# A hybrid attention and linear-attention block: low-rank weights loaded inside the gk unit, operand splits tied to their weight groups, thirteen bridging products, one more raw tile

## The chip, the cores and the metric

The kernel runs on one core of a Trainium2 chip. The metric is the device time of one execution in microseconds; lower is better. The core has five engines with instruction queues of their own: PE (matrix products), DVE (vector), ACT (activations, also copies and casts), POOL, and SP, which here only issues DMA transfers. They meet only through semaphores, and each queue is worked off in order, so an instruction that waits holds back all that stands behind it on its engine.

## The reference

One encoder layer over 512 tokens of width 2048. A normalised and modulated input goes through one projection; its columns feed a dilated window attention (16 heads of 64) and a bidirectional gated linear attention (GLA, 4 heads). Both branches are gated, concatenated and projected back:

```python
mod = jax.nn.silu(c) @ w_cond[layer] + b_cond[layer]
shift, scale, gate = jnp.split(mod, 3, axis=-1)
h = rms_norm(x) * (1.0 + scale[:, None]) + shift[:, None]
proj = h @ w_in[layer]
aq, ak, av, ag, gq, gk, gv, gg, lr_f, lr_b = jnp.split(proj, PROJ_SPLITS, axis=-1)
...                       # dilated attention of aq, ak, av in three patterns, merged
a_out = att.reshape(B, S, ATT_WIDTH) * jax.nn.silu(ag)
log_g_f = jax.nn.log_sigmoid(lr_f @ gla_gate_up_fwd[layer] + gla_gate_bias_fwd[layer]) / GLA_GATE_NORM
...                       # the same backward; chunked GLA of gq, gk, gv in both directions
g_out = rms_norm(o_fwd + o_bwd).reshape(B, S, GLA_WIDTH) * gla_norm_gain[layer] * jax.nn.silu(gg)
y = jnp.concatenate([a_out, g_out], axis=-1) @ w_out[layer]
x = x + gate[:, None] * y
return rms_norm(x) * final_gain
```

All of it is float32. `lr_f` and `lr_b` are the low-rank columns, 32 in all, from which the decay of the GLA is made.

## The kernel before, in words

**Split products.** A float32 product is made of three faster ones. Each weight tile and each activation tile is split into a high part (a rounding copy on ACT, names ending in `h` or `_hi`) and a low part (the difference, on DVE, ending in `l` or `_lo`). `three` (L230 to L232) issues high x high, high x low and low x high into one sum, so most of PE's work is rows of L230, L231 and L232.

**Stages, in order of time.** (1) Start, to about 107 us: while the conditioning weights (`cb`) and the first projection weights (`rawa`) arrive, `silu(c)` is spread over all partitions by small products on `pc` (L299). `warm` (L296) issues products on a constant tile `hot` whose results nobody reads: 5 before those products, 6 after them. Then come the first real products (`sta`, L591 for the first two of 16 blocks of 128 rows of the contraction, `three` after that); block k needs `h_hi` and `h_lo` of k (L534 on ACT, L537 on DVE), which need the sum over `cb` of k on DVE (L328). (2) Units `qk2`, `qk4`, `qk6`, `gk`: each projects a further group of columns, in 8 groups of weights, and runs the attention of four heads beside it, as "side work" given as pairs of a place (0 to 1 of the unit) and a function. A place of 1 or more spills into the next unit. (3) The value unit (`ps_gv`, weights `V0` to `V27`), whose products follow Strassen's scheme with seven instead of eight block products; `low_rank` (L1312, L1313) and the first GLA head run beside it. (4) Units `ag0`, `ag1`, `gg0`, `gg1` with the other GLA heads. (5) The output projection: two column pairs, seven products each (P1, P7, P6, P4, P5, P3, P2), every product in four weight groups, weights `O0` to `O55`. Its operands are A11, S3, S2, A22, S1, S4 and A12, which are sums and differences of parts of `cat[0..3]` and are split into high and low (`halves`, L1458 on ACT and L1459 on DVE).

**What sets the order.** PE stands in program order. The other engines' instructions are placed by a scheduler at build time; `tc.issue_after(x)` forbids it to place an instruction ahead of x, and a tile pool with n buffers makes the n-th next user of a tag wait until the oldest is released. The names below are used in what follows:

- `lrb` is the tile with the low-rank weights (L1303, a DMA issued by SP); `lrs` its split (L1306 on ACT, L1307 on DVE). `upr`/`ups` (L1320, L1326, L1327) are the up-projection of the decay and its split.
- `pth` and `ptl` are the split transposed attention weights (L888, L889; L906 and L908 for a rest block of 32 rows), `o` the attention values (L915), `gkt` the copies of the gk unit's sums out of PSUM (L1299).
- `GLA_FIRST` holds the places of the ten pieces of GLA head 0 in the value unit; pieces 7 and 8 are `outs(0)` and `outs(1)` (products `go`, L1123), piece 9 is `norm` (products `gn`, L1137, L1138).
- `to_s1`, `to_s2`, `to_s4` (L1471, L1474, L1477, all on DVE) turn parts of `cat` into S1, S2 and S4 in place.
- `later(pair, prod, g, go)` puts `go` into group g of a product of the output projection, ahead of its matrix products. `last["hi"]` and `last["lo"]` are the newest weight split on ACT and on DVE.
- `out_tile` gives the raw weight tiles of the output: even ones from the common ring of four, odd ones from `OUT_DEEP` on from a ring of three in the pool `op`.

Of the kernel before, what the change touches and what calls it, by code (L numbers as in the profile page):

```python
# [10 lines left out]
F32 = mybir.dt.float32  # L11
# [7 lines left out]
P = 128  # L19
S = 512  # L20
D = 2048
KT = D // P
# [96 lines left out]
TOKENS = [slice(256 * c + a, 256 * c + 256, 2) for a in range(2) for c in range(2)]  # L119

GLA_AT = (0.01, 0.02, 0.33, 0.46, 0.46, 0.56, 0.64, 0.76, 0.76, 0.88)
GLA_FIRST = (0.3, 0.38, 0.55, 0.62, 0.775, 0.81, 0.86, 0.9, 0.92, 0.97)

SUMS_IN = {"ag0": 8, "ag1": 8, "gg0": 8}

# [66 lines left out]
def block_kernel(ctx: ExitStack, tc: tile.TileContext, a: dict):  # L192
    nc = tc.nc
# [14 lines left out]
    def T2(name, dt=F32, parts=P):  # L208
        return t2.tile([parts, 512], dt, tag="t2", name=name)
# [34 lines left out]
    def small_inputs():  # L244
        nc.scalar.dma_start(cin, a["c"])
        nc.scalar.dma_start(bcond, a["bcond"])
# [4 lines left out]
    def cond_load(k, e):  # L251

        cb = B8(f"cb{k}_{e}", [2048])
        n = 4 if k == e == 0 else 1
        for z in range(n):
            w = 2048 // n
            nc.sync.dma_start(cb[:, w * z:w * z + w], a["wm"][k, e, :, w * z:w * z + w])
        cond_tiles[k, e] = cb
# [18 lines left out]
    def half_load(z):  # L277
        if not z:
            start_w["a", 0] = RAW("rawa0", [1024])
        c = slice(512 * z, 512 * z + 512)  # L280
        nc.sync.dma_start(start_w["a", 0][:, c], a["w_sa"][0, :, 0, c])
# [11 lines left out]
    def warm(n):  # L293

        for _ in range(n):
            mm(psw, hot[:, :P], hot, start=True, stop=True)  # L296
# [4 lines left out]
    with tc.manual_schedule(engines=PLANNED):  # L301
        small_inputs()
        cond_load(0, 0)
        half_load(0)
        x_load(0)
        half_load(1)
        nc.scalar.preload_act_table_set("silu_and_others")
        nc.vector.memset(hot.bitcast(F32), 1.0)
        nc.vector.memset(epst, EPS)
        nc.vector.memset(ch.bitcast(F32), 0.0)  # L310
        nc.vector.memset(sel.bitcast(F32), 0.0)
        nc.gpsimd.memset(cl.bitcast(F32), 0.0)
        warm(5)

        nc.vector.tensor_copy(ch[:4], cin[:, :512])
        act(sel[:4], cin[:, 512:], AF.Copy)
        tt(cl[:4], cin[:, :512], ch[:4].bitcast(F32), op=ALU.subtract)

        nc.vector.tensor_scalar(bcond[:, 16:32], bcond[:, 16:32], 1.0, None, op0=ALU.add)
        for j in range(4):  # L320
            spread(j, ch, True)
            spread(j, cl, False)
            act(sb[:, 512 * j:512 * j + 512], pcs[j], AF.Silu)
        warm(6)

    def cond_sum(dst, w, with_, init):

# [37 lines left out]
    raws, wts, low, last = {}, {}, set(), {}  # L365
# [27 lines left out]

    def out_tile(s, name):
        if s % 2 and s >= OUT_DEEP:
            return op.tile([P, 2, 512], F32, tag="raw", bufs=3, name=name)
        return RAW(name, [2, 512])

    second = {}
# [108 lines left out]
    part = cst.tile([P, 3], F32, tag="part", name="part")  # L508
# [146 lines left out]
    for z in range(2):  # L655
        c = slice(512 * z, 512 * z + 512)
# [36 lines left out]
    for k in range(2):  # L693
        for z in range(2):
            for e in (0, 2, 1):
                name = ("mm", "a", k, 7) if (z, e) == (1, 1) else ("m", k, z, e)
# [3 lines left out]
    for i in range(n):  # L700
        if i > 15:
            mm_task(i)
        st, k, j = chain[i]
# [14 lines left out]
    for i in range(n, 2 * n):  # L718
        mm_task(i)
        st, k, j = chain[i]  # L720
# [3 lines left out]
    for w in range(4):  # L724
        for kt in range(4):
            j, g = w // 2 * 4 + kt, w % 2
# [285 lines left out]
    def gla_head(h):  # L1012
# [135 lines left out]

        at = GLA_AT if h else GLA_FIRST
        return list(zip(at, [gates(0), gates(1), turn(0), turn(1), states(0), states(1), att,  # L1150
# [8 lines left out]
    def unit(name, natural, side=(), lr=None):  # L1159
        side = sorted(spill + list(side) + block_sums(name), key=lambda x: x[0])  # L1160
        spill[:] = [(at - 1, go) for at, go in side if at >= 1]
        side = [x for x in side if x[0] < 1]
        ps = [PJ(f"ps_{name}_{i}") for i in range(4)]
        pos, tick, ticks = 0, 0, 64
        for g in range(KT // 2):
            i0 = gi[name, g]
            split_hi(i0)
            split_hi(i0 + 1)
            for ahead in (2,) if name in SUMS_IN or name == "gg1" else (2, 3):
                fetch(i0 + ahead)  # L1170
            split_lo(i0)
            hi, lo = wts[i0]
            for i in range(4):
                for kk in range(2):
                    k = 2 * g + kk
                    rh, rl = h_hi[:, k, :], h_lo[:, k, :]
                    if natural:
                        t = slice(i * P, i * P + P)
                        cw = slice(kk * 512, kk * 512 + 512)
                        three(ps[i], rh[:, t], rl[:, t], hi[:, cw], lo[:, cw], k == 0, k == KT - 1)  # L1180
                    else:
                        c = slice(kk * 512 + i * P, kk * 512 + i * P + P)
                        three(ps[i], hi[:, c], lo[:, c], rh, rl, k == 0, k == KT - 1)
                    tick += 1
                    if tick % 8 == 2:
                        split_lo(i0 + 1)
                    while pos < len(side) and side[pos][0] * ticks <= tick:
                        urgent(side[pos][1])
                        pos += 1
                if lr is not None:  # L1190
                    lr(4 * g + i)
        while pos < len(side):
            urgent(side[pos][1])
            pos += 1
        return ps
# [93 lines left out]
    for n, p in (("qk2", 0), ("qk4", 2), ("qk6", 4)):  # L1289
        ps = unit(n, False, attention((p, p + 1)) + ([(0.05, shift_row)] if p == 2 else []))  # L1290
        for q in range(2):
            qk_evict(p + 2 + q, ps[2 * q], ps[2 * q + 1])

    ps = unit("gk", False, attention((6, 7)))
    kp_.close()
    gs = mid.enter_context(tc.tile_pool(name="gs", bufs=1, reuse_waits="tile"))
    gla["k"] = B8("gkt", [4, 512])
# [1 line left out]
        act(gla["k"][:, i, :], ps[i], AF.Copy)  # L1299


    lrb = T2("lrb")
    nc.sync.dma_start(lrb.rearrange("p (k c) -> p k c", k=KT), a["w_lr"][0])  # L1303
    lrs = gp.tile([P, KT, 2, 32], F32R, tag="g", name="lrs")
    lrb3 = lrb.rearrange("p (k c) -> p k c", k=KT)
    act(lrs[:, :, 0, :], lrb3, AF.Copy)  # L1306
    tt(lrs[:, :, 1, :], lrb3, lrs[:, :, 0, :].bitcast(F32), op=ALU.subtract)  # L1307
    plr = PA("plr")
# [126 lines left out]
    for j in range(2):  # L1435
        ps = unit(f"ag{j}", False, gla_head(1 + j) + some_sums(f"ag{j}"))
        gate_evict(ps, cat[j], f"a{j}", vbias[:, 4 * j:4 * j + 4])
    ps = unit("gg0", False, gla_head(3) + some_sums("gg0"))
# [5 lines left out]
    def part(z, c):  # L1444

        return cat[z][:, :, half[c]]
# [6 lines left out]
    def halves(name, z, src):  # L1453

        hi, lo = (t[:, 4 * z:4 * z + 4, :] for t in ops[name])

        def go():
            act(hi, src, AF.Copy)  # L1458
            tt(lo, src, hi.bitcast(F32), op=ALU.subtract)  # L1459
        return go  # L1460
# [9 lines left out]
    def to_s1(z):  # L1470
        tt(part(z, 1), part(2 + z, 1), part(z, 1), op=ALU.subtract)  # L1471

    def to_s2(z):
        stt(part(z, 0), part(z, 1), -1.0, part(z, 0), op0=ALU.mult, op1=ALU.subtract)  # L1474

    def to_s4(z):
        tt(part(z, 0), part(2 + z, 0), part(z, 0), op=ALU.add)  # L1477
# [3 lines left out]
            (0.65, lambda: to_s1(0)), (0.8, lambda: to_s2(0))]  # L1481
    ps = unit("gg1", False, side + some_sums("gg1"))
    gate_evict(ps, cat[3], "g1")
    to_s1(1)
    to_s2(1)
    mid.close()
    op = ctx.enter_context(tc.tile_pool(name="op", bufs=1, reuse_waits="tile"))
    for e in "hl":
# [145 lines left out]
    def later(pair, prod, g, go):  # L1634
        todo.setdefault((pair, prod, g), []).append(go)

    def product(pair, prod, ps, first, last, rows=(0, 1)):

        ah, al = ops[with_[prod]]
        for g in range(4):  # L1640
            s = (pair * len(OUT_ORDER) + OUT_ORDER.index(prod)) * 4 + g
            i0 = gi["O", s]
            ahead = 0 in rows
            if ahead:
                split_hi(i0)
                split_hi(i0 + 1)
                for n in (2, 3, 4, 5):
                    fetch(i0 + n)
                whole(i0 + 2)
                split_lo(i0)  # L1650
                for go in todo.get((pair, prod, g), ()):
                    go()
            wh, wl = wts[i0]
            for n in rows:
                t = slice(P * n, P * n + P)
                for kk in range(2):
                    k = 2 * g + kk
                    c = slice(512 * kk, 512 * kk + 512)
                    three(ps[n], ah[:, k, t], al[:, k, t], wh[:, c], wl[:, c],
                          first and k == 0, last and k == 7, not first)  # L1660
                if ahead and n == 0:
                    split_lo(i0 + 1)

    def a12():
        operand("A12", [B8(f"A12{e}", [4, 512], F32R) for e in "hl"])

    for z in range(2):
        later(0, "P1", 2 * z, halves("S2", z, part(z, 0)))
        later(0, "P7", 2 * z, halves("A22", z, part(2 + z, 1)))
        later(0, "P6", 2 * z, halves("S1", z, part(z, 1)))  # L1670
        later(0, "P6", 2 * z + 1, lambda z=z: (to_s4(z), halves("S4", z, part(z, 0))()))
    later(0, "P4", 0, a12)
    for z in range(2):
        later(0, "P4", 1 + 2 * z, lambda z=z: halves("A12", z, part(2 + z, 0))())
# [133 lines left out]
```

## Time and profile before

| | |
|---|---|
| median of 3 runs | 905.48 us (905.13 to 906.01) |
| the profiled execution | 907.22 us, of which the span from first to last instruction is 905.4 us |
| mean granted TensorE clock | 0.996 |
| PE busy | 890.0 us of the span (98%) |
| DVE, ACT, POOL busy | 731.2, 491.6, 125.9 us |
| DMA | 242.33 MB, mean 268 GB/s |

In the rows of the profile a time stands in microseconds from the span's start, then the duration, the engine (PEld is PE's weight load, SPq the queue of SP), the line, the operation, the tiles as out<-in, their shape, the number of instructions put together (x4), and in brackets the idle time of the engine ahead of the row with what ended it. The start of the next product tells the pace of PE: products overlap, and the duration of one is longer than the step to the next.

### The profile page before, as it was taken

How to read it: one execution, taken by the hardware profiler on the slowest of the kernel's cores; microseconds unless marked ns; L12 is line 12 of the kernel's file. 1: busy time of each engine (PE TensorE's matmuls, PEld its weight loads, DVE VectorE, ACT ScalarE, POOL GpSimd, SP SyncE). 2: the span in 40 equal slices, each digit the busy share in tenths (PEclk: the TensorE clock that was granted, in tenths of full speed). 3: DMA queues.
4: the chain of work that ended last, by engine and by line, in shares of the span. 5: the costliest groups of instructions: out<-in, count | busy, mean ns of one | idle time of the engine just before them, and what ended most of it. 6: DMA issues, size and time to landing. Idle time of an engine off the chain costs nothing.

```text
span 905.4 us, 12339 instructions
## 1 busy us (share of the span) xinstructions
PE 890.0 (98%) x4159; PEld 739.2 (82%) x4159; DVE 731.2 (81%) x1220; ACT 491.6 (54%) x841; POOL 125.9 (14%) x219
## 2 busy tenths in 40 slices
PE   8999999999999999999999999999999999999996
PEld 6888788888888888887778888888888888888885
DVE  7998799878989989888568668595787559797687
ACT  5554533466655745655657554373664248455454
POOL 0000000023323333243000101112020100000001
PEclk9999999999999999999999999999999999999999
DMA  9999489398798898998778879778796988777863
GB/s 342 401 411 363 186 344 367 134 306 226 202 266 273 247 265 247 249 298 223 232 260 255 311 206 308 206 249 262 231 279 208 275 286 289 282 288 249 289 238 154
DMA packets 65547, 242.33 MB, mean 268 GB/s; under 512 B 9190, under 2 KB 11526, under 8 KB 55883
## 3 DMA queue, kind: packets, MB, share of 16 engines
q1 hardware_dynamic: 58724, 199.23, 61.5%
q0 software_dynamic: 6464, 42.01, 19.4%
q8 instruction: 33, 0.54, 0.2%
q10 hardware_dynamic: 296, 0.30, 0.1%
q14 instruction: 30, 0.25, 0.1%
HBM read 224.64 MB, written 51.47 MB: 305 GB/s over the span
## 4 chain that ended last, share of the span: by engine, by line
PE 91%; DVE 3%; ACT 2%; DMA 2%; issue 1%; SPq 0%; DVEq 0%; ACTq 0%
PE ps_qk L230 5%; PE ps_qk L232 5%; PE ps_qk L231 5%; PE g L232 4%; PE g L230 4%; PE g L231 4%; PE stb L232 3%; PE stb L231 3%; PE stb L230 3%; PE ps_ag L232 3%; PE ps_ag L230 3%; PE ps_ag L231 3%; PE o L915 3%; PE sta L230 3%; PE sta L231 3%; PE sta L232 3%
## 5 line engine op out<-in xcount | busy, mean ns | idle before, releaser
L864 POOL TENSOR_SCALAR p<-p,st 128x32 f32<-128x32 f32 (+2 forms) x108 | 59.8, 565 | 159.9 <-DVE st L854 91.2
L328 DVE CUSTOM_DVE_ANT_0 cb<-cb,sb,c_bcond 128x2048 f32<-128x2048 f32 (+1 forms) x32 | 73.4, 2295 | 1.9 <-DMA cb<-in_wm 1.6
L851 ACT ACTIVATE p<-p,st 128x416 f32<-128x416 f32 x64 | 41.0, 641 | 49.2 <-DVE st L847 42.3
L429 POOL DMA_DIRECT2D T<-in_w_o x32 | 23.2, 725 | 159.4 <-ACT V2h L493 14.8
L888 ACT ACTIVATE pth<-t 128x384 fp32r<-128x384 f32 x64 | 31.0, 485 | 19.8 <-PE t L882 11.1
L889 DVE TENSOR_TENSOR ptl<-t,pth 128x384 fp32r<-128x384 f32 x64 | 35.2, 551 | 5.2 <-ACT pth L888 3.7
L882 PE MATMUL t<-c_ident,p 128*128 128x128 f32 x192 | 31.3, 272 | 0.0
L882 PEld LDWEIGHTS t<-c_ident,p 128*128 128x128 f32 x192 | 24.3, 139 | 7.9
L847 DVE CUSTOM_DVE_ANT_0 p<-s,g,st 128x256 f32<-128x256 f32 x64 | 27.7, 432 | 1.8
L847 DVE CUSTOM_DVE_ANT_0 p<-s,g 128x160 f32<-128x160 f32 x64 | 23.5, 367 | 4.2 <-PE s L840 3.5
L328 DVE CUSTOM_DVE_ANT_0 rawg<-rawg,crow,gate 128x1024 f32<-128x1024 f32 x16 | 20.4, 1279 | 4.0 <-DMA rawg<-in_wg 4.0
L1581 POOL TENSOR_SCALAR x<-x,rn 128x512 f32<-128x512 f32 x2 | 2.3, 1167 | 148.5 <-ACT rn L1570 148.5
L429 POOL DMA_DIRECT2D T3V<-in_w_gv x8 | 5.5, 687 | 125.1 <-ACT qk21h L493 118.7
L839 PE MATMUL s<-ks,qh 128*128 128x416 f32 x64 | 22.6, 353 | 0.0
L906 ACT ACTIVATE pth<-r 32x128 fp32r<-32x128 f32 x64 | 17.2, 269 | 9.9 <-PE r L899 4.5
L840 PE MATMUL s<-ks,ql 128*128 128x416 f32 x64 | 22.4, 350 | 0.0
L1091 ACT ACTIVATE sq<-st,sc 128x256 f32<-128x256 f32 x24 | 12.2, 506 | 18.6 <-DVE st L1081 10.0
L328 DVE CUSTOM_DVE_ANT_0 rawg<-rawg,crow,c_bcond 128x1024 f32<-128x1024 f32 x16 | 20.3, 1279 | 0.5 <-DVE g L1028 0.5
L429 POOL DMA_DIRECT2D T<-T x16 | 9.1, 571 | 79.9 <-ACT V8h L493 12.9
L915 PE MATMUL o<-pth,vv 128*128 128x512 f32 (+1 forms) x64 | 15.9, 369 | 2.2 <-DVE pth L908 1.1
L466 DVE TENSOR_TENSOR raw_O<-raw_O,raw_P 128x1024 f32<-128x1024 f32 x8 | 9.8, 1225 | 10.1 <-DMA raw_O<-in_w_o 7.8
L568 ACT ACTIVATE h_hi<-xt,shift 128x512 fp32r<-128x512 f32 x16 | 11.5, 721 | 10.3 <-DVE shift L328 9.5
(1661 smaller groups left out, 3151.6 us busy)
## 6 DMA issues: line engine op xcount, KB each, us to landing
cb<-in_wm SPq DMA_DIRECT2D x31, 1024.0 KB, 9.3
T<-in_w_o POOLq DMA_DIRECT2D x32, 512.0 KB, 6.5
rawg<-in_wg SPq DMA_DIRECT2D x32, 512.0 KB, 5.4
raw_O<-in_w_o SPq DMA_DIRECT2D x32, 512.0 KB, 4.6
raw_qk<-in_w_qk SPq DMA_DIRECT2D x24, 512.0 KB, 4.9
raw_O<-T SPq DMA_DIRECT2D x24, 512.0 KB, 5.0
rawb<-in_w_sb SPq DMA_DIRECT2D x16, 512.0 KB, 8.9
rawv<-in_wv SPq DMA_DIRECT2D x16, 512.0 KB, 5.6
```

What stands on the lines that cost most here:

```text
L230: mm(ps, lh, rh, start=first, stop=False, skip_group_check=more)
L231: mm(ps, ll, rh, start=False, stop=False, skip_group_check=more)
L232: mm(ps, lh, rl, start=False, stop=last, skip_group_check=more)
L328: return nc.vector.tensor_tensor_reduce(out=w, in0=w, in1=with_, op0=ALU.mult, op1=ALU.add, scale=1.0, scalar=init, accum_out=dst)
L429: move = nc.gpsimd.dma_start(dst, src, max_dma_last_dim=8192, **how).ins
L847: top = nc.vector.tensor_tensor_reduce(out=t[:, lo:hi], in0=ps[:, lo:hi], in1=gt[h][:, at:at + 2 * (hi - lo) - 1:2], op0=ALU.add, op1=ALU.min,
L851: act(t, t, AF.Exp, bias=st[:, 0:1], scale=-1.0, accum_out=st[:, 1:2])
L864: last["pool"] = nc.gpsimd.tensor_scalar(to, of, st[:, 2:3], 1.0, op0=ALU.mult, op1=ALU.mult).ins
L882: nc.tensor.transpose(pk[:, n_ * P:n_ * P + P], t[:, first_ + kt * P:first_ + kt * P + P], ident)
L888: act(hi, src, AF.Copy)
L889: tt(lo, src, hi.bitcast(F32), op=ALU.subtract)
L915: mm(po[:, P * a0:P * a1], vv[h // 4][:, c, h % 4, :], pt[:, at:at + (a1 - a0 - 1) * step + 1:step, :], start=n_ == z == 0, stop=False, sk ...
```

## The change

Five edits:

1. `warm(6)` becomes `warm(13)`: thirteen products on `hot` follow the spread products instead of six.
2. `lrb` is loaded by a piece of side work at place 0.88 of the gk unit, not behind the unit.
3. In `GLA_FIRST`, `outs(0)` moves from 0.9 to 0.91 and `outs(1)` from 0.92 to 0.93.
4. In the output, `to_s1(1)` and `to_s2(1)` move from ahead of the output into groups 2 and 3 of P1, and the splits of S2, A22, S1 and S4 go through `in_turn`, which places them behind the newest weight split of both engines; the two splits of S2 move to group 1 of P1 and group 1 of P7.
5. The ring of odd raw tiles has four buffers instead of three.

```diff
-GLA_FIRST = (0.3, 0.38, 0.55, 0.62, 0.775, 0.81, 0.86, 0.9, 0.92, 0.97)
+GLA_FIRST = (0.3, 0.38, 0.55, 0.62, 0.775, 0.81, 0.86, 0.91, 0.93, 0.97)
...
-        warm(6)
+        warm(13)
...
-            return op.tile([P, 2, 512], F32, tag="raw", bufs=3, name=name)
+            return op.tile([P, 2, 512], F32, tag="raw", bufs=4, name=name)
...
-    ps = unit("gk", False, attention((6, 7)))
+    lrb = []
+
+    def lr_load():
+        lrb.append(T2("lrb"))
+        nc.sync.dma_start(lrb[0].rearrange("p (k c) -> p k c", k=KT), a["w_lr"][0])
+
+    ps = unit("gk", False, attention((6, 7)) + [(0.88, lr_load)])
...
-    lrb = T2("lrb")
-    nc.sync.dma_start(lrb.rearrange("p (k c) -> p k c", k=KT), a["w_lr"][0])
...
     gate_evict(ps, cat[3], "g1")
-    to_s1(1)
-    to_s2(1)
...
+    def in_turn(pair, prod, g, *fns):
+
+        def go():
+            with tc.issue_after(last["hi"]), tc.issue_after(last["lo"]):
+                for fn in fns:
+                    fn()
+        later(pair, prod, g, go)
...
+    in_turn(0, "P1", 2, lambda: to_s1(1))
+    in_turn(0, "P1", 3, lambda: to_s2(1))
     for z in range(2):
-        later(0, "P1", 2 * z, halves("S2", z, part(z, 0)))
-        later(0, "P7", 2 * z, halves("A22", z, part(2 + z, 1)))
-        later(0, "P6", 2 * z, halves("S1", z, part(z, 1)))
-        later(0, "P6", 2 * z + 1, lambda z=z: (to_s4(z), halves("S4", z, part(z, 0))()))
+        in_turn(0, ("P1", "P7")[z], 1, halves("S2", z, part(z, 0)))
+        in_turn(0, "P7", 2 * z, halves("A22", z, part(2 + z, 1)))
+        in_turn(0, "P6", 2 * z, halves("S1", z, part(z, 1)))
+        in_turn(0, "P6", 2 * z + 1, lambda z=z: to_s4(z), halves("S4", z, part(z, 0)))
```

The edits leave PE's order as it was but for the seven further `warm` products and the place of `go`. What the scheduler makes of them on the other engines, at the places of which the prediction speaks:

**End of the gk unit, SP.** `S` is a store of a token sum, `raw_V` the weight tiles V5 and V6. Before:

```order
L391 DMA raw_V_4347<-in_w_gv 128x1024
L1320 DMA upr<-in_up 128x1024
L1220 DMA S_1506<-S_4100 128x512
L391 DMA raw_V_4384<-in_w_gv 128x1024
L1303 DMA lrb<-in_w_lr 128x512
```

And now:

```order
L391 DMA raw_V_4354<-in_w_gv 128x1024
L1324 DMA upr<-in_up 128x1024
L1220 DMA S_1513<-S_4107 128x512
L1298 DMA lrb<-in_w_lr 128x512
L391 DMA raw_V_4391<-in_w_gv 128x1024
```

The load of `lrb` has changed places with the load of V6, which waits for a raw buffer.

**The same place, ACT.** Before:

```order
L1299 ACTIVATE gkt_4325<-ps_gk_3671 128x512
L888 ACTIVATE pth<-t_4277 128x3x128
L1299 ACTIVATE gkt_4325<-ps_gk_3672 128x512
L888 ACTIVATE pth<-t_4286 128x3x128
L906 ACTIVATE pth<-r_4296 32x128 x2
L1306 ACTIVATE lrs<-lrb 128x16x32
L888 ACTIVATE pth<-t_4306 128x3x128
L906 ACTIVATE pth<-r_4296 32x128 x2
L1299 ACTIVATE gkt_4325<-ps_gk_3673 128x512
L1326 ACTIVATE ups<-upr 128x1024
L1299 ACTIVATE gkt_4325<-ps_gk_3674 128x512
```

And now:

```order
L1305 ACTIVATE gkt_4334<-ps_gk_3678 128x512
L888 ACTIVATE pth<-t_4286 128x3x128
L1310 ACTIVATE lrs<-lrb 128x16x32
L1305 ACTIVATE gkt_4334<-ps_gk_3679 128x512
L888 ACTIVATE pth<-t_4295 128x3x128
L1330 ACTIVATE ups<-upr 128x1024
L906 ACTIVATE pth<-r_4305 32x128 x2
L888 ACTIVATE pth<-t_4315 128x3x128
L1305 ACTIVATE gkt_4334<-ps_gk_3680 128x512
L1305 ACTIVATE gkt_4334<-ps_gk_3681 128x512
L906 ACTIVATE pth<-r_4305 32x128 x2
```

`lrs` stands three rows earlier, `ups` has moved ahead of the last attention tile, and the second pair of `pth<-r` stands behind two more `gkt` copies.

**Start of the output, DVE.** `cat<-cat,sgg` are the gates of the last unit; of the rows of shape 128x4x256, the one that reads `cat_5127` is `to_s4(0)` and the one that reads `cat_5990` is `to_s1(1)` (now the one with `cat_5997`); the SCALAR_TENSOR_TENSOR is `to_s2(1)`. Before:

```order
L1202 TENSOR_TENSOR cat_5990<-cat_5990,sgg_6780 128x512
L1459 TENSOR_TENSOR c_l<-cat_1611,c_h 128x1024
L1202 TENSOR_TENSOR cat_5990<-cat_5990,sgg_6783 128x512
L1477 TENSOR_TENSOR cat_1611<-cat_5127,cat_1611 128x4x256
L1471 TENSOR_TENSOR cat_3027<-cat_5990,cat_3027 128x4x256
L477 TENSOR_TENSOR O2l<-raw_O_6807,O2h 128x1024
L1474 SCALAR_TENSOR_TENSOR cat_3027<-cat_3027 128x4x256
L477 TENSOR_TENSOR O3l<-raw_O_6809,O3h 128x1024
```

And now:

```order
L1202 TENSOR_TENSOR cat_5997<-cat_5997,sgg_6787 128x512
L1202 TENSOR_TENSOR cat_5997<-cat_5997,sgg_6790 128x512
L477 TENSOR_TENSOR O2l<-raw_O_6812,O2h 128x1024
L1463 TENSOR_TENSOR c_l<-cat_1618,c_h 128x1024
L1475 TENSOR_TENSOR cat_3034<-cat_5997,cat_3034 128x4x256
L477 TENSOR_TENSOR O3l<-raw_O_6814,O3h 128x1024
L1478 SCALAR_TENSOR_TENSOR cat_3034<-cat_3034 128x4x256
L477 TENSOR_TENSOR O4l<-raw_O_6816,O4h 128x1024
```

Three rows of operand work that stood ahead of the split `O2l` now stand behind it or later.

More of the change, by code (lines that the diff above doesn't have):

```diff
@@ L1299, in block_kernel @@
         act(gla["k"][:, i, :], ps[i], AF.Copy)
-    lrb = T2("lrb")
-    nc.sync.dma_start(lrb.rearrange("p (k c) -> p k c", k=KT), a["w_lr"][0])
     lrs = gp.tile([P, KT, 2, 32], F32R, tag="g", name="lrs")
-    lrb3 = lrb.rearrange("p (k c) -> p k c", k=KT)
+    lrb3 = lrb[0].rearrange("p (k c) -> p k c", k=KT)
     act(lrs[:, :, 0, :], lrb3, AF.Copy)
```

## Prediction

> **What bounds the kernel now.** I read the page first (busy shares, then the chain of waits), then what PE waited for, then PE's own timeline for every step longer than its usual one, and at each of these places the rows of the engine that released PE.
>
> ```profile
> PE 890.0 (98%) x4159; PEld 739.2 (82%) x4159; DVE 731.2 (81%) x1220; ACT 491.6 (54%) x841; POOL 125.9 (14%) x219
> ...
> PE 91%; DVE 3%; ACT 2%; DMA 2%; issue 1%; SPq 0%; DVEq 0%; ACTq 0%
> ```
>
> PE holds the end: busy for 98% of the span, 91% of the chain that ended last. No edit takes a product away that the reference needs, so only time in which PE stands or runs slowly can be saved. From the list of waits (us in total, times, longest):
>
> ```profile
> PE sta L591 <- ACT h_hi L534: 2.7, 1, 2.7
> ...
> PE o L915 <- DVE pth L908: 1.1, 1, 1.1
> ...
> PE o L915 <- ACT pth L888: 1.0, 1, 1.0
> ```
>
> The first and the third lie where the change works; the second (near 418) is left as it is. The fourth loss is the clock. Stretches of PE alone (start:end, length, busy time and products, granted clock, DMA share, GB/s):
>
> ```profile
> 7.87:11.27 3.40, 1.02 (x4) 1.00 1.02 405
> 11.28:14.69 3.41, 3.41 (x10) 0.50 1.03 429
> 441.36:444.76 3.40, 2.45 (x12) 1.00 0.06 24
> ```
>
> After a stretch with PE busy for 1.02 of 3.40 us (30%) the clock was 0.50 for 3.41 us. A stretch with 2.45 of 3.40 (72%) was followed by no fall.
>
> **The change part by part. Thirteen `warm` products.** The rows of the start:
>
> ```profile
> 6.08 1.52 PE L296 MATMUL warm<-hot 128*128 128x512 f32 x6
> ...
> 9.67 0.94 ACT L534 ACTIVATE h_hi<-xt,scale 128x256 fp32r<-128x256 f32 x2
> 10.25 1.21 PE L591 MATMUL sta<-sa0hi,h_hi 128*128 128x512 f32 x4 [2.65 <-ACT h_hi L534]
> 11.28 1.90 PE L591 MATMUL sta<-sa0lo,h_hi 128*128 128x512 f32 x4
> ...
> 14.68 1.09 PE L591 MATMUL sta<-sa0hi,h_hi 128*128 128x512 f32 x4
> 15.55 0.94 ACT L534 ACTIVATE h_hi<-xt,scale 128x256 fp32r<-128x256 f32 x2
> 17.44 1.07 PE L591 MATMUL sta<-sa1hi,h_hi 128*128 128x512 f32 x4
> 21.20 0.74 DVE L537 SCALAR_TENSOR_TENSOR h_lo<-xt,scale,h_hi 128x512 fp32r<-128x512 f32 x1
> 23.10 0.39 PE L231 MATMUL sta<-sa2hi,h_lo 128*128 128x512 f32 x1
> ```
>
> Twelve products at full clock took 14.68 to 17.44, 0.23 each. Seven more `warm` cost 7 x 0.23 = 1.61 us of PE time, and six end at 6.08+1.52 = 7.60, so thirteen end at 9.21. `h_hi` releases the first real product at 10.25 as before; 1.04 us of cover is left, so the cost is nothing, and that excludes a loss here. If `h_hi` came a microsecond sooner, each further 0.23 us would be paid.
>
> The gain is the clock. The stretch 7.87 to 11.27 would then hold 1.02 + (9.21-7.87) = 2.36 us of work, 69%: next to the 72% after which the clock stayed, far from the 30% after which it fell. Without the fall the eight products from 11.28 to 14.68 take 8 x 0.23 = 1.84 instead of 3.40, 1.56 less. Not all of it can be kept, as x arrives no faster. The second `h_hi` is whole at 15.55+0.94 = 16.49, its first half near 16.02, against 17.44-1.56 = 15.88 for the first product on it: a wait of about 0.15. The second low half ends at 21.20+0.74 = 21.94 and its first reader stands at 23.10: 1.16 us is the most by which PE can be early there, 1.11 with the 0.05 us or so from an engine's end to PE's start. I take 1.1 us; the bounds are 0 (the clock falls anyway) and 1.16. Nothing behind it takes it back, since from there on the stage is paced by PE.
>
> The Trainium skill (TensorE: Matmul & The Clock Gate, Part 1, the clock gate) has the clock fall after at least one idle window of 3413 ns. By that rule a gap of 2.65 us should not have lowered it; this trace disagrees with that (0.50 after 30% busy), though its 3.41 us of half speed agree with the window's length. The same part says that the windows run freely and shift from run to run; no run shown here tells that. By the first rule these products would be worth 0, by the trace 1.1 us.
>
> **`lrb` in the gk unit.**
>
> ```profile
> 428.69 0.33 SPq L1220 DMA_DIRECT2D S<-S  x1
> 434.11 0.33 SPq L391 DMA_DIRECT2D raw_V<-in_w_gv  x1
> 434.49 0.64 SPq L1303 DMA_DIRECT2D lrb<-in_w_lr  x1
> 436.40 0.48 ACT L888 ACTIVATE pth<-t 128x384 fp32r<-128x384 f32 x1
> ...
> 440.92 0.39 PE L232 MATMUL ps_gv_P<-V0l,h_hi 128*128 128x512 f32 x1
> 441.12 0.63 ACT L1306 ACTIVATE lrs<-lrb 128x512 fp32r<-128x512 f32 x1 [2.78 <-DMA lrb<-in_w_lr]
> 441.77 0.49 ACT L888 ACTIVATE pth<-t 128x384 fp32r<-128x384 f32 x1
> 442.29 0.56 ACT L906 ACTIVATE pth<-r 32x128 fp32r<-32x128 f32 x2
> 442.31 1.13 PE L915 MATMUL o<-pth,vv 128*128 128x512 f32 x4 [1.01 <-ACT pth L888]
> 442.87 0.60 ACT L1299 ACTIVATE gkt<-ps_gk 128x512 f32<-128x512 f32 x1
> 443.36 1.05 ACT L1326 ACTIVATE ups<-upr 128x1024 fp32r<-128x1024 f32 x1
> 444.31 0.59 ACT L1299 ACTIVATE gkt<-ps_gk 128x512 f32<-128x512 f32 x1
> 444.44 1.22 DVE L1327 TENSOR_TENSOR ups<-upr,ups 64x1024 fp32r<-64x1024 f32 x1 [0.75 <-ACT ups L1326]
> ```
>
> SP stood from 429.02 to 434.11 at the load of V6, which waits for a raw buffer; `lrb` behind it landed 441.12-434.49 = 6.63 us after its issue, and ACT waited 2.78 us for it with the last attention tile's `pth` queued behind. PE, due at 440.92+0.23 = 441.15, began `o` at 442.31: 1.16 us lost. Now `lrb` goes out at about 429.02 and lands near 435.65; the issue takes 0.64, long over when V6's buffer comes free at 434.11, so V6 loses nothing.
>
> ACT's new order puts `lrs` behind the `pth` of 436.40, at 436.88. From the starts above, its steps are `lrs` 0.65, `pth` 0.52, two `r` 0.58, `gkt` 0.49, `ups` 0.95. In the new order `lrs`, `gkt`, `pth`, `ups`, two `r` and the last tile's `pth` come to 0.65+0.49+0.52+0.95+0.58+0.52 = 3.71, ending near 440.59: in time for 441.15. Behind it stand two `gkt` (0.98) before the last two `r`, whose first is done at 440.59+0.98+0.29 = 441.86. PE's second product of `o` reads it, due one step later, at about 441.40: so a wait of 0.46 takes the place of 1.16, a saving of 0.70 us. By durations instead of steps (0.63+0.60+0.49+1.05+0.56+0.49+1.20+0.28 = 5.30) that `r` is done at 442.18, the wait 0.78, and 0.38 is left. DVE's 1.22 for `ups` stands ahead of its share of `r` too, but in the shade of 0.98 of `gkt`. I take the steps, since ACT's instructions follow one another so here: 0.7, between 0 and 1.16.
>
> **`outs` later.**
>
> ```profile
> 524.30 0.69 DVE L1108 SCALAR_TENSOR_TENSOR at<-c_ident,at 128x512 f32<-128x512 f32 x1
> 525.13 0.46 PE L1123 MATMUL go<-at,gv 128*128 128x128 f32 x2 [0.28 <-ACT V27h L493]
> 533.97 0.69 DVE L1136 TENSOR_TENSOR gsl<-gsq,gsh 128x512 fp32r<-128x512 f32 x1 [0.70 <-ACT gsh L1135]
> 535.42 0.39 PE L1138 MATMUL gn<-gsl,ones 128*128 128x512 f32 x1
> ```
>
> The bracket names a weight split, but `at` ended at 524.99, just before PE went on: that is what `go` waits for, and PE's step there is 0.44 us too long. Three products of 0.23 ahead of `go` cover it: -0.44. The same shift reaches the norm behind it: `gsl` ended at 534.66, 0.76 before its reader; 0.68 later leaves 0.08. I take -0.4, bounds 0 and -0.44; if `gsl` slips by another tenth it costs that tenth.
>
> **Output splits at their groups.**
>
> ```profile
> 746.61 1.22 DVE L1477 TENSOR_TENSOR cat<-cat,cat 128x1024 f32<-128x1024 f32 x1
> 746.63 1.06 ACT L493 ACTIVATE O2h<-raw_O 128x1024 fp32r<-128x1024 f32 x1
> 748.88 1.22 DVE L477 TENSOR_TENSOR O2l<-raw_O,O2h 128x1024 fp32r<-128x1024 f32 x1
> 749.63 0.39 PE L231 MATMUL g<-O2h,A11l 128*128 128x512 f32 x1
> 750.15 0.50 PE L232 MATMUL g<-O2l,A11h 128*128 128x512 f32 x1
> ```
>
> `O2l` waited behind `to_s4(0)` and `to_s1(1)` on DVE, and its reader started 0.52 after the product before it instead of 0.23: 0.29 lost. Now nothing stands between the gates and `O2l`; even if `O2h` is no earlier it can run from 747.69 to 748.91, 0.95 ahead of PE's 749.86. -0.3, bounds 0 and -0.4 (the step behind it is slow too). `to_s1(1)`, `to_s2(1)` (1.22 each on DVE) and the two splits moved later are paid from idle DVE and ACT time, which the shares above say there is; where one of them comes in front of a weight split by mistake the price is a rival below. The fourth raw tile costs memory alone: 0.
>
> **Sum.** -1.1 -0.7 -0.4 -0.3 = -2.5 us. On the profiled execution (907.22, of which span 905.4) that gives 904.7; it lies 1.74 above the median of the runs, and the same step from 905.48 gives 903.0, 0.28% faster. About 0.2% (1.8 us) is what a measurement of this kernel can tell from no change.
>
> **Rivals.**
>
> *The thirteen products change nothing in the runs that are timed.* For it: one profiled execution shows one phase of the clock's stretches; were the gap of 2.65 us cut in two by a border, each part would hold about 60% work and the clock might not fall even before. The profiled execution is 1.74 us above the median, about one such fall (1.56). Against it: nothing shows a run without the fall. It takes 1.1 from the sum: 904.1. It is also what the rule of an idle window gives.
>
> *`lrb` frees ACT and the last attention tile waits as long as before.* `ups` and two `gkt` (0.95+0.98) now stand ahead of what PE reads; with DVE's 1.22 for `ups` in the way of its part, the 0.7 goes: 903.7. Against it: 0.38 is left even by durations.
>
> *Splits collide in the output.* An operand split or a sum of 1.22 us on DVE lands in front of a weight split that had less spare time than that: 1.2 to 2.4 us, 904.2 to 905.4. For it, `O2l` before; against it, `in_turn` puts them behind the newest weight split.
>
> *Slower: `lrb` lands late with the whole tile queued behind it.* Place: ACT's `lrs`, now three rows earlier. From `lrs` at 436.88 to the first `r` at 441.86 is 4.98 us of queue, and PE's second product of `o` stood near 442.6 before (442.31 and a step); so each microsecond that `lrb` lands after 437.65 makes PE later than before, one for one. The other parts give 1.8: slower than before from a landing at 439.45 (10.4 us after issue), measurably from 441.3 (12.2 us), 907.3. The 6.63 us and the idle DMA (share 0.06 here) speak against it.
>
> **How the numbers follow.** Forecast 0.58, with a range of its own of 902.1 to 903.6; no effect of the thirteen 0.24; nothing from `lrb` 0.10; a collision 0.05; `lrb` late 0.03. The low end takes the upper bounds of all terms together with a little of other waits, 1.16+1.16+0.44+0.4 = 3.16, 902.3, widened by the 0.4 that the runs shown differ from their median: 901.9. The high end takes in the second case with the same 0.4 (904.5) and leaves out the collisions and the late load. Faster by over 0.2%: the forecast, half of the third case, a sixth of the second, 0.67; slower 0.04; the rest 0.29.
>
> **What would show it.** Right: a granted clock of 1.00 from 11.28 on, `sta` on the second tile near 16.1 and PE early by about 1.1 at 23; `lrs` near 436.9 less that, without a wait for DMA, and `o` with a short wait on ACT's or DVE's `r`; no idle time ahead of the first `go` of 525; steps of 0.23 around `O2l`. Wrong: a 0.50 stretch again near 11, or PE back in its old place by 30; a long wait for `lrb`; new waits of PE for a weight split in the output; a wait for `gsl`.

## The result, and the profile after

The changed kernel takes 903.75 us (median of 22 runs, 903.17 to 904.81) where the kernel before takes 905.08 (22 runs, 904.0 to 906.01): a ratio of 0.9986 with a 95% interval of 0.9981 to 0.9992, 1.3 us. It is faster, by half of what was forecast (0.14% instead of 0.28%), and inside the 0.2% below which the prediction spoke of no change. One execution each of the ring kernel and the turns kernel below ran near 1117 us at a granted clock of 0.75, and their ratios leave it out.

The two profiled executions say something else: 907.22 and 903.61 us, spans 905.4 and 901.8, a difference of 3.6 us. PE's place in the two, by the rows of before and after: 1.75 us apart behind the first stage (95.64 and 93.89), 2.69 behind the late `o` (444.21 and 441.52), 3.15 ahead of `O2l` (749.63 and 746.48), 3.57 behind it (750.50 and 746.93). The four places thus gave back 1.7, 1.0, 0.5 and 0.4: all that was lost there, but for 0.2 to 0.3 us ahead of the late `o`. In the medians only 1.3 of these 3.6 are left, and that is what the experiments are about.

The page and the list of PE's waits of the changed kernel:

```profile
PE 890.3 (99%) x4166; PEld 740.2 (82%) x4166; DVE 731.1 (81%) x1220; ACT 492.8 (55%) x841; POOL 126.2 (14%) x219
...
PE 90%; DVE 4%; ACT 3%; issue 1%; DMA 1%; DVEq 0%; SPq 0%; ACTq 0%
```

```profile
PE warm L296 <- DVE hot L308: 1.5, 1, 1.5
PE o L915 <- DVE pth L908: 1.1, 1, 1.1
```

Of the waits of PE only the one that the change does not touch is left (and the first, for the very first tile). PE's start, in which the thirteen products stand:

```profile
4.30 0.68 PE L299 MATMUL pc<-c_lo,sel 128*128 128x512 f32 x1
4.77 0.63 PE L299 MATMUL pc<-c_hi,sel 128*128 128x512 f32 x1
5.20 0.63 PE L299 MATMUL pc<-c_lo,sel 128*128 128x512 f32 x1
...
6.93 3.11 PE L296 MATMUL warm<-hot 128*128 128x512 f32 x13
10.11 1.20 PE L591 MATMUL sta<-sa0hi,h_hi 128*128 128x512 f32 x4
11.14 1.08 PE L591 MATMUL sta<-sa0lo,h_hi 128*128 128x512 f32 x4
```

The clock did not fall: four products took 1.08 us behind 11 us instead of 1.90. But there is a second difference: the bridging products began at 6.93, not at 6.08, because the spread products before them still ran at a step of 0.43 (4.77 to 5.20) in this execution. The thirteen end at 10.04, with no cover left, not at 9.21.

The places of `lrb` (SP's issue, ACT's new order, PE), of `outs` and of the output:

```profile
427.38 0.39 SPq L1298 DMA_DIRECT2D lrb<-in_w_lr  x1
...
434.68 0.49 ACT L888 ACTIVATE pth<-t 128x384 fp32r<-128x384 f32 x1
435.05 0.63 ACT L1310 ACTIVATE lrs<-lrb 128x512 fp32r<-128x512 f32 x1
...
438.10 0.49 ACT L888 ACTIVATE pth<-t 128x384 fp32r<-128x384 f32 x1
438.48 1.08 ACT L1305 ACTIVATE gkt<-ps_gk 128x512 f32<-128x512 f32 x2
439.19 0.39 PE L232 MATMUL ps_gv_P<-V0l,h_hi 128*128 128x512 f32 x1
439.42 1.33 PE L915 MATMUL o<-pth,vv 128*128 128x512 f32 x4
439.59 0.56 ACT L906 ACTIVATE pth<-r 32x128 fp32r<-32x128 f32 x2
```

```profile
521.60 0.69 DVE L1108 SCALAR_TENSOR_TENSOR at<-c_ident,at 128x512 f32<-128x512 f32 x1
522.45 0.39 PE L232 MATMUL ps_gv_P<-V25l,vS 128*128 128x512 f32 x1
522.67 0.38 PE L1123 MATMUL go<-at,gv 128*128 128x128 f32 x2
531.41 0.69 DVE L1136 TENSOR_TENSOR gsl<-gsq,gsh 128x512 fp32r<-128x512 f32 x1 [0.70 <-ACT gsh L1135]
532.16 0.51 PE L1138 MATMUL gn<-gsl,ones 128*128 128x512 f32 x1
```

```profile
743.86 1.23 DVE L477 TENSOR_TENSOR O2l<-raw_O,O2h 128x1024 fp32r<-128x1024 f32 x1 [1.68 <-ACT O2h L493]
746.48 0.39 PE L231 MATMUL g<-O2h,A11l 128*128 128x512 f32 x1
746.71 0.39 PE L232 MATMUL g<-O2l,A11h 128*128 128x512 f32 x1
```

ACT reads `lrb` without a wait, the last tile's `pth` is ready at 438.59, ahead of PE's 439.42, and the first four products of `o` take 0.2 us more than the 1.13 of before: that is all that is left of the wait. `go` follows its predecessor by 0.22. `gsl` ends at 532.10, 0.06 ahead of its reader. `O2l` is ready 1.6 us ahead of its reader.

### The profile page after: what moved, and what is told of

It reads as the page before. It is cut to its first block, busy times and chain, and to the rows that moved or that the text cites. A ratio compares the mean times of both kernels' runs of the same rounds, so it can differ in the third digit from the quotient of the medians.

```text
span 901.8 us, 12359 instructions
## 1 busy us (share of the span) xinstructions
PE 890.3 (99%) x4166; PEld 740.2 (82%) x4166; DVE 731.1 (81%) x1220; ACT 492.8 (55%) x841; POOL 126.2 (14%) x219
## 4 chain that ended last, share of the span: by engine, by line
PE 90%; DVE 4%; ACT 3%; issue 1%; DMA 1%; DVEq 0%; SPq 0%; ACTq 0%
PE ps_qk L232 5%; PE ps_qk L230 5%; PE ps_qk L231 5%; PE g L231 4%; PE g L232 4%; PE g L230 4%; PE stb L232 3%; PE stb L230 3%; PE stb L231 3%; PE ps_ag L230 3%; PE ps_ag L231 3%; PE ps_ag L232 3%; PE sta L232 3%; PE sta L230 3%; PE sta L231 3%; PE ps_gv_P L231 3%
## 5 line engine op out<-in xcount | busy, mean ns | idle before, releaser
L1359 DVE TENSOR_TENSOR vS<-rawS,vS 128x1024 fp32r<-128x1024 f32 x8 | 9.7, 1223 | 8.5 <-ACT vS L1358 8.4
```

## The experiments

Four kernels make one part of the change each (edits 4 and 5 together); they ran on one chip beside the kernel before (905.25 us).

**The thirteen products alone** (the orders of ACT, DVE and SP are those of before, row for row):

```diff
-        warm(6)
+        warm(13)
```

> The kernel before with thirteen bridging products instead of six, nothing else. The sum of the prediction: 1.1 us faster in every run, from the clock's fall that goes. Theory of the phase: the stretches in which the clock is set lie at another place in each execution, so that the gap behind six products lowers the clock only in some of them; then the median gains 0 to 0.6 us, while single runs gain up to 1.7, and the spread of the runs becomes smaller. Theory of the two profiles alone: 1.7 us, the difference of the two traces at 96 us.

Measured: 905.12 us, ratio 1.0002 (0.9992 to 1.0011). No gain; the 1.1 us of the prediction lies outside the interval.

**The load of `lrb` alone** (the diff of edit 2).

> The kernel before with only the load of lrb moved into the gk unit. The prediction: 0.7 us faster. The two profiles alone: 1.0 us (PE is 1.73 us ahead behind the attention tile before it and 2.71 behind it). If the landing of lrb varies from run to run: less than 0.5. The profile also shows one more execution of the start with six products: by the theory of the phase PE's clock need not fall near 11 us in it, by the prediction it falls.

Measured: 905.15 us, ratio 1.0 (0.9991 to 1.0008). The profile shows ACT without a wait for the load, as in the changed kernel, and yet there is no gain in the median; an effect under 0.8 us cannot be told from none with this spread.

**`outs` alone.**

```diff
-GLA_FIRST = (0.3, 0.38, 0.55, 0.62, 0.775, 0.81, 0.86, 0.9, 0.92, 0.97)
+GLA_FIRST = (0.3, 0.38, 0.55, 0.62, 0.775, 0.81, 0.86, 0.91, 0.93, 0.97)
```

> The kernel before with only the two outs of the GLA at 0.91 and 0.93. The prediction: 0.4 us faster (0.45 by the two profiles), no wait for go at 525, gsl 0.08 us ahead of its reader. The rival: a wait for gsl takes part of it back, 0 to 0.3 faster. One more execution of the start with six products, as above.

Measured: 905.2 us, ratio 1.0001 (0.9992 to 1.0009). The wait for `go` is gone in the profile; by the median, inconclusive.

**The output alone** (edits 4 and 5).

> The kernel before with only the output's operands and splits at their groups and the fourth raw tile. The prediction: 0.3 us faster (0.4 by the two profiles). The rival: splits collide elsewhere in the output in some runs, 0 or slower by up to 1.2. One more execution of the start with six products, as above.

Measured: 904.33 us, ratio 0.999 (0.9982 to 0.9999): 0.9 us faster (0.1 to 1.6), more than the 0.3 of the prediction in the middle, and the runs lie closer together (903.36 to 905.15).

None of the four profiles had the clock's fall, though three of them have six bridging products. So the next question was put the other way round: the whole change without the thirteen.

```diff
-        warm(13)
+        warm(6)
```

> The changed kernel with six bridging products again, the other four edits kept. Theory of the phase: the thirteen are worth nothing in most executions, so this is as fast as the change, 1.0 to 1.6 us faster than the kernel before; in its profile the clock need not fall near 11 us, and PE reaches the last tile of the first stage within 0.5 us of the changed kernel's time. The prediction: 1.1 us slower than the change, so about as fast as before (0.3 faster), with a clock of 0.50 near 11 us.

Measured: 903.64 us, ratio 0.9978 (0.9968 to 0.9988), at least as fast as the change (0.9986, 0.9981 to 0.9992). And the kernel before without any bridging product:

```diff
-        warm(6)
```

> The kernel before without any bridging product behind the spread products. PE's slow pace at the very start (a product every 0.43 us) ended between 4.5 and 7.5 us in the ten executions so far, and the spread products with it between 6.1 and 7.3; without the six, PE then stands for 2.3 to 4 us. Theory of the phase: some stretch of 3.41 us then holds under 40% of work in nearly every execution, the clock falls to 0.50 behind it, and the median is 0.8 to 1.6 us above the kernel before. Theory that the fall is always there already (the prediction's): no change, 0 to 0.2. Theory that a fall costs nothing, as x arrives late anyway: a clock of 0.50 in the profile and no change.

Measured: 906.71 us, ratio 1.0012 (1.0003 to 1.0022): 1.1 us slower by the ratio (0.3 to 2.0), 1.4 by the medians. Its stretches of PE (start:end, length, busy time and products, granted clock), and its rows:

```profile
7.07:10.48 3.41, 0.71 (x4) 0.99 1.05 402
10.48:13.89 3.41, 3.41 (x10) 0.51 1.02 419
```

```profile
6.91 0.44 PE L299 MATMUL pc<-c_lo,sel 128*128 128x512 f32 x1
10.04 1.78 PE L590 MATMUL sta<-sa0hi,h_hi 128*128 128x512 f32 x4 [2.70 <-ACT h_hi L533]
```

So a fall of the clock is dear, as the prediction had it, and six products already prevented it in the profiles of the parts. The change and the kernel before were run once more, the latter for its profile alone.

> The changed kernel once more, for a comparison on one chip with the kernel that holds gk7's low split back and has six bridging products. 1.0 to 1.6 us faster than the kernel before; a wait of PE of about 1.1 us near 417, no wait near 440 beyond 0.3, none ahead of go and none in the output.

Measured: 903.89 us, ratio 0.9986 (0.9977 to 0.9994). In its profile PE waits 1.1 us near 417, as expected, and otherwise only at the start.

> The kernel before once more, for its profile alone. By the theory of the phase the place at which PE leaves its slow pace decides the start: if that is later than about 5 us, no clock of 0.50 near 11 us and a wait for h_hi under 2 us; if it is near 4.5, as in the first profile, the fall and 2.6 us. The wait for lrb's tile near 440 is anything from 0 to 1.4 us, go and O2l cost 0.44 and 0.4 us as in each profile of these two orders. By the prediction: the fall, and 1.1 us near 442.

Measured: 905.18 us. Its start:

```profile
4.76 0.63 PE L299 MATMUL pc<-c_hi,sel 128*128 128x512 f32 x1
5.19 0.63 PE L299 MATMUL pc<-c_lo,sel 128*128 128x512 f32 x1
...
7.32 1.67 PE L296 MATMUL warm<-hot 128*128 128x512 f32 x6
9.72 1.18 PE L591 MATMUL sta<-sa0hi,h_hi 128*128 128x512 f32 x4 [0.72 <-ACT h_hi L534]
```

This is the very kernel of the prediction, and here the six products begin 1.24 us later and PE waits 0.72 us for `h_hi`, not 2.65. All profiled starts together, ordered by where the bridging products began (us; `pss` is the start of the second product of that line near 95, the end of the first stage):

| kernel | bridging | begins | wait for `h_hi` | clock behind it | `pss` |
|---|---|---|---|---|---|
| before | 6 | 6.08 | 2.65 | 0.50 | 96.06 |
| thirteen alone | 13 | 6.09 | 0.79 | 1.00 | 94.58 |
| change again | 13 | 6.16 | 0.72 | 1.00 | 94.21 |
| gk7 held, six (below) | 6 | 6.46 | 2.31 | 1.00 | 94.55 |
| `outs` alone | 6 | 6.65 | 1.59 | 1.00 | 93.99 |
| gk7 held (below) | 13 | 6.65 | 0.10 | 1.00 | 94.78 |
| turns (below) | 6 | 6.84 | 1.48 | 1.00 | 94.35 |
| output alone | 6 | 6.85 | 1.36 | 1.00 | 94.12 |
| change | 13 | 6.93 | 0.07 | 1.00 | 94.31 |
| change with six | 6 | 7.15 | 0.97 | 1.00 | 93.88 |
| `lrb` alone | 6 | 7.29 | 1.39 | 1.00 | 95.02 |
| ring (below) | 6 | 7.31 | 0.75 | 1.00 | 94.77 |
| before again | 6 | 7.32 | 0.72 | 1.00 | 94.59 |
| none | 0 | (7.35) | 2.70 | 0.51 | 95.84 |

The clock fell in only one of nine executions with six products, the one in which PE left its slow pace first. The mean of `pss` is 94.59 with six and 94.47 with thirteen, and 94.41 with six where the clock held. The rest of the spread goes with the moment at which `h_hi` is ready: where the clock held, PE's first product on it starts earliest in the change with six (9.65) and latest in `lrb` alone (10.43), and these two have the lowest and the highest `pss`, 93.88 and 95.02.

Why the clock held is seen by cutting the start into stretches of 3.41 us from where the steps fall from 0.43 to 0.23 (4.45 us in the profile before, where its trace also has the first record of a granted clock of 1.00; 4.7 in thirteen alone and in the change again, 7.75 in `lrb` alone). The emptiest stretch holds 1.02 us of work before and 0.71 with none, and there the clock fell; in the eight other executions with six it holds from 1.86 (gk7 held, six, shown below) to 2.69, and there it stayed. Thirteen alone and the change again left the slow pace nearly as early as the profile before, and hold 2.62 and 2.69; an estimate from these, less seven products of 0.23, is 1.0 to 1.1 with six.

**The output's two halves.** The ring of four alone, and the turns, meant to be alone with the ring of three. The first:

```diff
-            return op.tile([P, 2, 512], F32, tag="raw", bufs=3, name=name)
+            return op.tile([P, 2, 512], F32, tag="raw", bufs=4, name=name)
```

> The kernel before with only the fourth odd raw tile in the output. The prediction: 0, memory alone. Rival from the profiles of the parts (DVE waits 8.4 to 12.3 us for raw tiles in the output without the fourth tile, 3.6 to 4.3 with it): the loads go out earlier, the waits of DVE for raw_O and raw_P fall below 5 us, and 0.3 to 0.8 us are gained in the median, from the executions in which a late tile reaches PE.

Measured: 905.03 us beside 905.64 of before, ratio 0.9994 (0.9985 to 1.0004): inconclusive. SP's transfers stand in another order from 764 us on, DVE's waits for `raw_O` and `raw_P` fell to 3.7 us, as the rival said, and `O2l` cost what it did before.

> The kernel before with only the operands and splits at their groups, and the ring of three odd raw tiles. The prediction: 0.3 us faster, all of the output's gain. Rival of the ring: 0.4 from O2l alone, and DVE still waits 8 us or more for raw tiles, with waits of PE for O17l or O45l in some executions.

This kernel is not what its expectation says. Beside the turns, its edit cuts another ring, the common ring of raw tiles, from which the weights of the units before the output come too, from four to three:

```diff
-        return wp.tile([P] + shape, F32, tag="raw", bufs=4, name=name)
+        return wp.tile([P] + shape, F32, tag="raw", bufs=3, name=name)
```

Measured: five runs of 913.16 to 921.85 us, ratio 1.0129 (1.0104 to 1.0155), which neither theory had. The loss is not in the output, which begins 14 us later than in the kernel before run again. By this kernel's list of waits it lies in the GLA for the most part:

```profile
PE go L1123 <- DVE at L1108: 2.9, 1, 2.9
...
PE gn L1137 <- ACT gsh L1135: 1.4, 1, 1.4
...
PE s L839 <- DVE ptl L889: 1.0, 1, 1.0
```

SP's transfers stand in another order from 174 us on, at the loads for the qk units, long before the output, and ACT's and DVE's rows from about 456. With the waits for `go` and `gn` the clock fell to 0.50 too, for 6.83 and 3.41 us. So this kernel tells neither what the turns are worth nor anything of the ring of odd tiles; the turns alone were not measured.

What the output's edits do is better seen in the profiles. DVE's waits for raw tiles, in us, times and longest, in the kernel before and in the changed one:

```profile
DVE raw_O L466 <- DMA raw_O<-in_w_o: 7.8, 4, 3.2
DVE raw_O L466 <- DMA raw_P<-in_w_o: 2.2, 3, 1.8
```

```profile
DVE raw_O L466 <- DMA raw_O<-in_w_o: 3.1, 3, 2.0
DVE raw_O L466 <- DMA raw_P<-in_w_o: 0.5, 2, 0.3
```

and where such a wait reaches PE, in the kernel with `lrb` alone, which has the output of before:

```profile
863.65 1.23 DVE L466 TENSOR_TENSOR raw_O<-raw_O,raw_P 128x1024 f32<-128x1024 f32 x1 [2.57 <-DMA raw_O<-in_w_o]
864.79 1.22 DVE L477 TENSOR_TENSOR O45l<-raw_O,O45h 128x1024 fp32r<-128x1024 f32 x1
...
865.56 0.39 PE L231 MATMUL g<-O45h,c_l 128*128 128x512 f32 x1
866.06 0.50 PE L232 MATMUL g<-O45l,c_h 128*128 128x512 f32 x1
```

PE's step there is 0.50 instead of 0.23. Steps beyond the usual in the output come to 0.41 (before), 0.41, 1.32, 0.52, 0.41 and 0.94 us (before again) in the six profiles with the old output, and to nothing in all six with the new one and its ring of four. With the ring of four alone they come to 0.41, all of it at `O2l`.

**A version that beats both.** The one longer wait of PE that all the profiles so far share behind the start, near 417, is for a rest part of the head before, `pth`, on DVE. In the changed kernel:

```profile
413.48 1.23 DVE L477 TENSOR_TENSOR gk7l<-raw_gk,gk7h 128x1024 fp32r<-128x1024 f32 x1
...
415.44 0.69 DVE L1243 TENSOR_TENSOR S<-S,h_lo 128x512 f32<-128x512 f32 x1
416.17 0.28 DVE L908 TENSOR_TENSOR pth<-r,pth 32x128 fp32r<-32x128 f32 x1
...
416.60 1.05 PE L915 MATMUL o<-pth,vv 128*128 128x512 f32 x4 [1.11 <-DVE pth L908]
```

PE does not read the split of gk7 before 429.91, and yet it stands ahead of this part. It was held back:

```diff
-                    tt(low_, of, up.bitcast(F32), op=ALU.subtract)
+                    last["rest"] = tt(low_, of, up.bitcast(F32), op=ALU.subtract).ins
...
-            last["lo"] = tt(lo, raw, hi.bitcast(F32), op=ALU.subtract).ins
+            with tc.issue_after(last["rest"]) if groups[i] == ("gk", 7) else nullcontext():
+                last["lo"] = tt(lo, raw, hi.bitcast(F32), op=ALU.subtract).ins
```

> The changed kernel with the low split of gk7 (1.23 us on DVE) held until the last low rest part of the head before; it stood ahead of that part, for which PE waits 1.1 us in every profile so far, near 417. If that split is the whole of the wait, PE saves 1.1 us there and the median is 0.8 to 1.1 us below the change (2.1 to 2.4 below the kernel before). If the sum of 0.69 us that also stands ahead still holds PE, 0.4 to 0.7. If the parts behind it become late instead (p of the next tile, gk7 itself): 0.

Measured: 902.68 us (902.37 to 903.26), ratio 0.9972 (0.9961 to 0.9983), 0.96 us below the change with six on the same chip. The rows:

```profile
415.51 0.28 DVE L909 TENSOR_TENSOR pth<-r,pth 32x128 fp32r<-32x128 f32 x1
415.90 1.21 DVE L478 TENSOR_TENSOR gk7l<-raw_gk,gk7h 128x1024 fp32r<-128x1024 f32 x1
```

```profile
415.53 0.40 PE L232 MATMUL ps_gk<-h_lo,gk5h 128*128 128x512 f32 x1
415.94 1.05 PE L916 MATMUL o<-pth,vv 128*128 128x512 f32 x4
```

The split now stands behind the part, and PE goes on without a wait.

> The changed kernel with gk7's low split held back and six bridging products instead of thirteen. If that split was the whole of the wait near 417 and the thirteen are worth nothing: 0.8 to 1.1 us below the change on the same chip, 902.6 to 902.9 us. If the thirteen bring 1.1 us: no faster than the change.

Measured: 902.83 us (902.4 to 903.33), ratio 0.9973 (0.9964 to 0.9983), 1.06 below the change run on the same chip, with six bridging products. Its profile has the widest gap that did not lower the clock:

```profile
5.35:8.76 3.41, 2.66 (x12) 1.00 1.02 356
8.76:12.17 3.41, 1.86 (x8) 1.00 1.00 408
```

## Why the prediction came out so

**The thirteen products: wrong, and with it 1.1 of the 2.5 us.** The step that failed is "next to the 72% after which the clock stayed, far from the 30% after which it fell", taken as a statement on every run. It held for one execution. That the time came out in the stated range is in part luck: the range took in the case without these products, and the output gave more than was worked out (below). What came true is the first rival, "the thirteen products change nothing in the runs that are timed", whose 904.1 lies 0.35 from the result; its reason was half right. It named the border of the stretches, and in gk7 held, six, a border does cut a gap of 2.31 us in two. It lacked the other part: PE starts at a step of 0.43, and where it leaves that step, at such a border, lies anywhere from 4.45 to 7.75 us; the later it does, the later the six products end, and by the table the gap behind them is mostly shorter. The price of a fall was about right (none: 1.1 us, 0.3 to 2.0; 1.75 between the two profiles), its frequency was not: one in nine. By the three of fourteen starts that left the slow pace by 4.73, an estimate of what thirteen save is 1.5 us in about one execution of five, which the median does not show. The Trainium skill (TensorE: Matmul & The Clock Gate, Part 1, the clock gate) says that its windows run freely, so that the same kernel has a different number of slow products from run to run; these traces agree (the slow pace ended between 4.45 and 7.75 us). The prediction quoted it and gave the case no more than 0.24. Its other rule, a fall after a whole idle window, does not hold here: the clock fell behind 1.02 and 0.71 us of work in 3.41, and stayed behind 1.86.

Also wrong in kind, if harmless in size: "1.04 us of cover is left", which "excludes a loss". It was 0.07 in the changed kernel's profile. In before again the six began at 7.32 and ended at 8.99; seven more of 0.23 would end near 10.6, and PE went on with `h_hi` at 9.72 there. None of the four profiles with thirteen began so late, so a loss there is argued, not shown.

"x arrives no faster" was a draw too: the changed kernel's profile got 1.75 us out of a cap of 1.16.

**`lrb`: the mechanism right, the size half.** Predicted 0.7. The load's landing, 6.63 us in the profile before, was 4.9 to 6.9 us in the old place, and PE's idle time ahead of `o` with it: 1.01, 0, 1.34, 0.56, 0.19, 0.28 and 0 us in seven profiles with the old order and no other change there. In steps of PE the old order loses 0.60 on the mean and the new one 0.26 in all six profiles: 0.34. The remaining delay of PE's second product of `o` was forecast as 0.46 and is 0.26 (0.1 of it idle): ACT reached that `r` 0.27 us sooner than worked out (439.59+0.28 = 439.87, against 441.86 less the 1.72 us by which PE was ahead). So the step that failed here is to take one landing, 6.63 us, for every run.

**`outs`: right, by the profiles.** All seven profiles with the old places (the turns kernel aside) lose 0.44 at `go`; with the new ones nothing, but the step behind `gn` on `gsl` is 0.1 longer: 0.34 of the 0.4. `gsl` had a reserve of 0.06 us where 0.08 was worked out; that this is the reason is likely, not shown.

**The output: right at `O2l`, short elsewhere.** 0.41 in each old profile where 0.3 to 0.4 was said; the raw tiles' late arrivals, 0 to 0.9 us more by execution, were not seen, because the profile before happened to have none that reached PE. On the mean 0.67. "The fourth raw tile costs memory alone: 0" is the other step in doubt: with it alone the loads' order changed and DVE waited 3.7 us for raw tiles, against 7.6 to 12.3 in the six profiles with the old output; late tiles reached PE in three of these six and in none of the seven with the ring of four. What that is worth in time lies within the noise of the ring's own run.

**The sum** of these means, 0.12 + 0.34 + 0.34 + 0.67 = 1.5 us, agrees with the 1.3 measured (0.7 to 1.7 by the interval). The collision of splits and the late `lrb` did not come. These sizes come from profiles; alone, only the output's part was clear of the noise in the medians. What stays open: what the turns give alone, and why PE waited for `V21l`, behind the split of a reloaded token sum, in three of the seven profiles with the old `lrb` (0.21 to 0.82 us of steps, 0.2 on the mean of the seven, not in the sum) and in none of six with the new.

## What to carry to other kernels

A profile is one draw. Here a wait that ended with a DMA's landing (0 to 1.34 us ahead of `o`) and a clock that fell behind a gap had one size in that execution and another in the median; a wait that ended with an engine's queue had the same size in every profile of the same orders (0.44 at `go`, 0.41 at `O2l`). Before a stall is costed at its full length, ask which of the two ends it, and see how the profiled execution stands to the runs: here it was 2.1 us above their median, and its fall of the clock (`pss` 1.5 us behind the mean with six) and its long wait for `lrb` (0.6 above the mean) come to as much. The waits by queue order went away in the profiles in full, and gk7's split, the one that was large enough to time alone, paid in the median too (1.0 and 1.1 of 1.1).

## What the runs showed of the hardware

PE's slow start pace, a 128x512 product every 0.43 us, lasted until 4.45 us in one execution and 7.75 in another, although the row of granted clocks says 1.00 there; the steps of the products, not that row, tell it. One load of 128x512 at one place of one order landed 4.9 to 6.9 us after its issue. The clock fell to 0.50 behind stretches of 3.41 us in which PE was busy for 0.71, 1.02, 1.47 and 1.80 us (the last two in the turns kernel), and stayed at 1.00 behind 1.86 and, at the end of the kernel before (895.33 to 898.75), behind 1.59; so no one share of busy time, as the profile counts it, divides the two.
